# A hybrid decoder step on one core: sample and log-decay rows spread by DMA instead of one-hot matmuls, masks as Relu and 0/1 factors, squares added before their sum

## The chip, the core and the metric

The kernel runs on one core of one Trainium2 chip. The metric is the device time of one execution, in microseconds; the figure for the kernel before is the median of three runs.

## What is computed

One inference step of a two-layer decoder (D = 1024) for a prompt of 512 tokens and 8 samples of one token each. Each layer normalises x, makes one combined input projection, runs three recurrent branches on it (A: retention, B: mLSTM, C: SSD), gates and projects their sum back, then does cross-attention over 256 memory tokens and an MLP of width 4096. The prompt goes through the recurrences in chunks of 128 tokens; the samples are one state update and one read-out per head:

```python
# mLSTM, one chunk (retention has a constant decay, SSD has exp(cum_t - cum_s) in place of it)
logw = where(causal, b[t] - b[s] + i[s], -inf)
m_t  = maximum(b + m, max_s(logw))
sc   = (q @ k.T) * exp(logw - m_t)
num  = sc @ v + (q @ C) * exp(b + m - m_t)
C    = C * w_prev + (k * w_s).T @ v
# SSD, one chunk
seg  = where(causal, exp(cum_t - cum_s), 0)
y    = ((C_ @ B.T) * seg * dt_s) @ x + (C_ @ S.T) * exp(cum_t)
# a sample, each branch:  S = decay * S + v k^T ;  y = S q
```

The SSD output is multiplied by silu(z) and normalised by the mean of its squares over each group of 256 features. All arithmetic is fp32.

## The kernel before

**Layout and projections.** Activations lie feature-major: 128 features on the partitions, 520 columns (512 prompt tokens, 8 samples). Every large projection is done with fp32 split in a high and a low part. A weight chunk of 128 x 1024 (512 KB) is loaded into one of two `raw` buffers (L245), ScalarE copies its high part into `wh` (L255), VectorE subtracts to get `wl` (L256), and TensorE then runs 48 matmuls of 260 columns on it (`mmacc`, L169). `wh` and `wl` have two buffers each, so the split of a chunk starts when TensorE has finished the chunk two before it.

**Order of the work.** TensorE's order is written by hand. The mixer's per-head work sits in Python generators (`Stream`): `g_int_R`, `g_int_M`, `g_int_S` for the prompt (tile names with `Ri.`, `Mi.`, `Si.`), `g_smp_R`, `g_smp_M`, `g_smp_S` for the samples (`Rs.`, `Ms.`, `Ss.`). The projections pull them along: `mm()` advances a virtual clock by each matmul's length, and a generator that says `yield t` is resumed when that clock has moved by t microseconds. So a `yield` sets how much projection work TensorE does between two steps of a head. The other engines and the DMAs get their order from the tile scheduler's priorities. All DMAs, weights and states, loads and stores, are issued from SyncE's one queue (SP), in order; a DMA that has to wait holds up those behind it.

**Rows spread over partitions.** Three places need one row of numbers on all 128 partitions, and all three use TensorE with a one-hot stationary matrix (`sel`, `sel_b`, L629) that copies one row of the moving operand to all partitions of a PSUM tile:

- the decays. `RW` (L208) holds the rows -m_t of the four mLSTM heads and cum_t of the sixteen SSD heads, each as high and low part. `g_int_M` (L975 to L986) spreads a row over 512 columns, adds a mask of 0 and -1e30 by a second matmul (`idr`, `maskr`), and ScalarE makes exp of the sum with the s-term as bias; a third matmul of 384 columns feeds exp of the inter-chunk weight. `emask` in `g_int_S` (L1183 to L1192) does the first two for each of 4 heads of 4 groups. L1226 spreads two heads' rows over 64 partitions each with the table `selp`;
- the samples' q, k (or B, C) rows. `tok_rows` (L611 to L623) transposes two or four 128-column tiles, ScalarE and VectorE write high and low rows into `rows_r`, and for each sample a matmul spreads its 256 or 512 numbers (L806, L1073, L1288). VectorE then does, per sample and half, one `scalar_tensor_tensor` (state += v x k row) and one dot (state . q row), reading the row in PSUM;
- the SSD norm. `rms_cols` (L316) sums the squares of a group by matmuls with a column of ones, two 128-feature tiles one after the other.

Each layer has 4 heads in R, 4 in M, 4 groups of 4 heads in S, and 8 samples: 32 `emask` steps, 8 `g_int_M` heads, 16 pairs at L1226, 24 sample heads or groups, and 8 norms in the whole kernel.

Of the kernel before, what the change touches and what calls it, by code (L numbers as in the profile page):

```python
# [111 lines left out]
def tile_trunk(ctx: ExitStack, tc: tile.TileContext, I, O):  # L112
# [87 lines left out]
    mstage = tl(un, [128, 520], "row", 2)  # L200
    ld.dma_start(out=mstage[:, :128], in_=I["mask"])
    maskr = const.tile([128, 128], F32R, name="maskr")
    V.tensor_copy(out=maskr, in_=mstage[:, :128])
    idr = const.tile([128, 128], F32R, name="idr")
    V.tensor_copy(out=idr, in_=ident)

    sel = const.tile([128, 2, 32], F32R, name="sel")
# [216 lines left out]
    def layer(l, mp, load_x):  # L424
# [76 lines left out]
        def g_rows():  # L501
# [18 lines left out]
            V.tensor_scalar(out=RW[0:4, :], in0=mm_[:, 0:L], scalar1=-1.0, scalar2=None, op0=ALU.mult)  # L520
            V.scalar_tensor_tensor(out=RW[32:36, :], in0=mm_[:, 0:L], scalar=-1.0, in1=RW[0:4, :].bitcast(F32), op0=ALU.mult, op1=ALU.subtract)
# [1319 lines left out]
```

## Time and profile before

| | us |
|---|---|
| median of 3 runs (lowest, highest) | 3051.62 (3044.17, 3051.88) |
| the profiled execution | 3048.6 |
| its span from first to last instruction | 3046.8 |
| TensorE busy | 2987.1 (98%), 23708 matmuls |
| VectorE, ScalarE, GpSimd busy | 1909.3 (63%), 1241.2 (41%), 117.9 (4%) |
| DMA, queue of the loads and stores | 389.29 MB, 40.5% of 16 engines |

The chain of waits that ended last runs through TensorE for 94% of the span. The mixer, where the change lies, fills about 65 to 800 us and 1690 to 2550 us of the span. Two matmuls that follow each other overlap in the trace, so what one costs is read from start to start, not from its duration.

### The profile page before, as it was taken

The numbers are of one execution on the slowest core, as the hardware profiler recorded it, in microseconds if no ns is written. First come the engines' busy times: TensorE is split into PE (matmuls) and PEld (weight loads), VectorE is DVE, ScalarE is ACT, GpSimd is POOL, SyncE is SP. The second block draws the span as 40 slices with busy tenths as digits, with TensorE's granted clock in tenths as the row PEclk, the third lists the DMA queues.
The fourth block names the chain that finished last, engine by engine and source line by source line (L and its number), as shares of the span: only waits on it lengthen the run. The fifth ranks groups of instructions, "written<-read, shape, count | busy, mean of one in ns | idle before, by whom it ended". The sixth has DMA issues, their size and how long they took to land.

```text
span 3046.8 us, 57809 instructions
## 1 busy us (share of the span) xinstructions
PE 2987.1 (98%) x23708; PEld 2912.3 (96%) x23708; DVE 1909.3 (63%) x4460; ACT 1241.2 (41%) x2070; POOL 117.9 (4%) x384
## 2 busy tenths in 40 slices
PE   7999999999999999999999999999999999999998
PEld 7999999999999889999999999999999997899997
DVE  7677646766755765444577775567767557644445
ACT  5334444544433343322353454445444334332322
POOL 0001000100000000000000000000000000000000
PEclk9999999999999999999999999999999999999998
DMA  6334534433444642223353344444334446422322
GB/s 211 122 127 145 149 102 146 140 116 113 133 134 143 218 149 91 91 91 96 116 177 129 120 140 148 131 127 125 115 116 131 136 146 208 132 91 91 97 91 77
DMA packets 128537, 392.99 MB, mean 129 GB/s; under 512 B 16784, under 2 KB 27664, under 8 KB 128272
## 3 DMA queue, kind: packets, MB, share of 16 engines
q1 hardware_dynamic: 128272, 389.29, 40.5%
q8 instruction: 187, 3.06, 0.4%
q14 instruction: 78, 0.64, 0.1%
HBM read 331.68 MB, written 57.56 MB: 128 GB/s over the span
## 4 chain that ended last, share of the span: by engine, by line
PE 94%; DVE 2%; DMA 2%; ACT 1%; issue 0%; SPq 0%; ACTq 0%; DVEq 0%
PE mlp.pp L169 24%; PE br.pp L169 12%; PE Sp.pp L169 9%; PE Mp.pp L169 9%; PE Rp.pp L169 8%; PE br2.pp L169 6%; PE Si.pa L169 4%; PE out.pp L169 3%; PE Qp.pp L169 3%; PE wo.pp L169 3%; PE Mi.pa L169 3%; PE kv.pp L169 2%; PE Ap.pa L169 2%; PE Mp.pa L169 2%; PE Ri.pa L169 1%; PE Mi.pa L176 1%
## 5 line engine op out<-in xcount | busy, mean ns | idle before, releaser
L255 ACT ACTIVATE mlp.wh<-mlp.raw 128x1024 fp32r<-128x1024 f32 x127 | 134.8, 1061 | 485.5 <-PE mlp.pp L169 469.1
L169 PE MATMUL mlp.pp<-mlp.h,mlp.wh 128*128 128x260 f32 x2048 | 327.6, 282 | 0.0
L169 PE MATMUL mlp.pp<-kv.y,mlp.wh 128*128 128x260 f32 x1984 | 318.3, 282 | 0.0
L169 PEld LDWEIGHTS mlp.pp<-mlp.h,mlp.wh 128*128 128x128 f32 x2048 | 278.7, 188 | 0.0
L169 PEld LDWEIGHTS mlp.pp<-kv.y,mlp.wh 128*128 128x128 f32 x1984 | 270.2, 188 | 1.0 <-issue 1.0
L169 PE MATMUL mlp.pp<-mlp.h,mlp.wl 128*128 128x260 f32 x1024 | 205.0, 281 | 0.0
L169 PE MATMUL mlp.pp<-kv.y,mlp.wl 128*128 128x260 f32 x992 | 198.6, 281 | 0.0
L256 DVE TENSOR_TENSOR mlp.wl<-mlp.raw,mlp.wh 128x1024 fp32r<-128x1024 f32 x127 | 155.7, 1226 | 19.3 <-ACT mlp.wh L255 10.4
L1618 DVE SCALAR_TENSOR_TENSOR mlp.cc<-mlp.pp,rb.Cst 128x520 f32<-128x520 f32 x64 | 44.8, 700 | 188.3 <-PE mlp.pp L169 183.8
L169 PEld LDWEIGHTS mlp.pp<-mlp.h,mlp.wl 128*128 128x128 f32 x1024 | 157.4, 188 | 0.0
L169 PEld LDWEIGHTS mlp.pp<-kv.y,mlp.wl 128*128 128x128 f32 x992 | 152.5, 188 | 0.0
L169 PE MATMUL Rp.pp<-mlp.h,Rp.wh 128*128 128x260 f32 x736 | 120.5, 286 | 2.2 <-DVE Rp.ext L661 2.2
L256 DVE TENSOR_TENSOR Mp.wl<-Mp.raw,Mp.wh 128x1024 fp32r<-128x1024 f32 x56 | 68.5, 1224 | 85.2 <-ACT Mp.wh L255 85.2
L169 PE MATMUL Rp.pp<-h,Rp.wh 128*128 128x260 f32 x736 | 120.5, 286 | 1.3 <-DVE Rp.ext L661 1.3
L169 PE MATMUL Sp.pp<-mlp.h,Sp.wh 128*128 128x260 f32 x640 | 107.0, 290 | 0.0
L169 PE MATMUL Sp.pp<-h,Sp.wh 128*128 128x260 f32 x640 | 105.8, 288 | 0.0
L169 PEld LDWEIGHTS Rp.pp<-mlp.h,Rp.wh 128*128 128x128 f32 x736 | 101.1, 188 | 2.9 <-issue 2.4
L169 PE MATMUL Mp.pp<-mlp.h,Mp.wh 128*128 128x260 f32 x640 | 103.8, 284 | 0.0
L169 PE MATMUL Mp.pp<-h,Mp.wh 128*128 128x260 f32 x640 | 103.8, 284 | 0.0
L169 PEld LDWEIGHTS Rp.pp<-h,Rp.wh 128*128 128x128 f32 x736 | 101.1, 188 | 2.0 <-issue 1.5
L255 ACT ACTIVATE br.wh<-br.raw 128x1024 fp32r<-128x1024 f32 x64 | 67.6, 1056 | 82.8 <-PE br.pp L169 69.6
L1632 DVE TENSOR_TENSOR out.ucp<-mlp.pp,out.ucp 128x520 f32<-128x520 f32 x64 | 44.8, 700 | 80.6 <-PE mlp.pp L169 79.1
(799 smaller groups left out, 7981.3 us busy)
## 6 DMA issues: line engine op xcount, KB each, us to landing
mlp.raw<-wall SPq DMA_DIRECT2D x127, 512.0 KB, 3.4
br.raw<-wall SPq DMA_DIRECT2D x64, 512.0 KB, 3.5
Mp.raw<-wall SPq DMA_DIRECT2D x56, 512.0 KB, 3.5
Rp.raw<-wall SPq DMA_DIRECT2D x48, 512.0 KB, 3.5
Sp.raw<-wall SPq DMA_DIRECT2D x48, 512.0 KB, 3.5
kv.raw<-wall SPq DMA_DIRECT2D x33, 512.0 KB, 5.1
Ms.st<-s_ml SPq DMA_DIRECT2D x32, 512.0 KB, 3.5
o_mlC_s<-Ms.st SPq DMA_DIRECT2D x32, 512.0 KB, 2.9
```

The costliest lines, as they stand in the source:

```text
L169: PE.matmul(out, lhsT=lhsT, rhs=rhs, start=start, stop=stop)
L176: PE.transpose(out=out, in_=in_, identity=identity)
L255: A.activation(out=hi, in_=t, func=AF.Copy)
L256: V.tensor_tensor(out=lo, in0=t, in1=hi.bitcast(F32), op=ALU.subtract)
L1618: V.scalar_tensor_tensor(out=h2(rt), in0=ps, scalar=0.0, in1=h2(rbox[0]), op0=ALU.max, op1=ALU.mult)
L1632: V.tensor_tensor(out=h2(xs_.t[j]), in0=ps[:, :, :HF], in1=h2(xs_.t[j]), op=ALU.add)
```

## The change

Rows -m_t and cum_t are written to device memory (`rscr`) once per layer, and a DMA that repeats one row for 128 partitions (`row_bcast`, 256 KB into SBUF) takes the place of the one-hot matmul. ScalarE then does Relu of (row + bias), four times, and one Exp with scale -1; the mask is a factor 0/1, folded into `cbs` by VectorE for SSD, and applied by GpSimd's `affine_select` for mLSTM. A head's sample rows are written to device memory (`smp_scr`: one transpose of all, a copy by ScalarE, a DMA), and each `smp_bcast` DMA spreads 512 numbers of one row, or of two samples, over 128 partitions (256 KB, three buffers `bc`). VectorE reads them in SBUF. The rows of L1226 come by two DMAs of 64 partitions. The squares of SSD's two tiles are added by GpSimd before one round of `rms_cols`. The virtual-clock delays change with it. The attention's samples still use `tok_rows` and `sel_b`.

```diff
+    rscr = dram.tile([DEPTH, 20, L], F32, name="rscr")
+    sscr = dram.tile([DEPTH, 3, 4, NB * 512], F32, name="sscr")
+    def row_bcast(l, r, c0=0):
+        t = tl(un, [128, 512], "bcE", 2)
+        ld.dma_start(out=t[:, c0:L], in_=rscr[l, r, c0:L].partition_broadcast(128))
+        return t
...
+        def smp_scr(kind, h, src, n, scale=1.0):
+            ps = pa()
+            tr(out=ps[:, 0:128], in_=src, identity=ident)
+            rt = tl(sm, [128, 128], "rowt", 2)
+            A.activation(out=rt[0:NB * n, :], in_=ps[0:NB * n, 0:128], func=AF.Copy, scale=scale)
+            st_.dma_start(out=sscr[l, kind, h, 0:NB * n * 128].rearrange("(r f) -> r f", f=128), in_=rt[0:NB * n, :])
+        def smp_bcast(kind, h, b0, nb, w):
+            t = tl(un, [128, nb, w], "bc", 3)
+            ld.dma_start(out=t.rearrange("p a b -> p (a b)"), in_=sscr[l, kind, h, b0 * w:(b0 + nb) * w].partition_broadcast(128))
+            return t
...
@@ g_smp_R @@
-            r = tok_rows(qks)
+            smp_scr(0, h, qkw, 2)
...
-            yield 3.69
+            bcs = [smp_bcast(0, h, 2 * q, 2, 256) for q in range(2)]
+            yield 7.0
...
@@ g_int_M @@
-            ps = pa([128, NC, 128])
-            mm(ps.rearrange("p a b -> p (a b)"), lhsT=sel_b(h), rhs=RW, start=True, stop=False)
-            mm(ps, lhsT=idr, rhs=maskr.unsqueeze(1).to_broadcast([128, NC, 128]), start=False, stop=True)
+            mb = row_bcast(l, 16 + h)
+            yield 2.5
             E = tl(un, [128, NC, 128], "E", 2)
             for c in range(NC):
-                A.activation(out=E[:, c, :], in_=ps[:, c, :], func=AF.Exp, bias=colT[:, c, 0, h:h + 1])
-            wb = pa()
-            mm(wb[:, 0:384], lhsT=sel_b(h), rhs=RW[:, 128:512], start=True, stop=True)
+                A.activation(out=E[:, c, :], in_=mb[:, c * C:(c + 1) * C], func=AF.Relu, bias=colT[:, c, 0, h:h + 1])
+            A.activation(out=E, in_=E, func=AF.Exp, scale=-1.0)
+            G.affine_select(out=E, in_=E, pattern=[[0, NC], [1, C]], compare_op=ALU.is_ge, fill=0.0, base=0, channel_multiplier=-1)
...
@@ g_smp_M @@
+            smp_scr(1, h, qkmw[:, h * 32:h * 32 + C], 4)
             while h and not msmps[h - 1].done:
                 yield 0.5
-            r = tok_rows([t[:, (2 * h + i) * NB:(2 * h + i) * NB + C] for t in (qmw, kmw) for i in range(2)])
...
-            yield 2.3
+            bcs = [smp_bcast(1, h, b, 1, 512) for b in range(2)]
+            yield 7.0
...
-                    bc = pa()
-                    mm(bc, lhsT=sel_b(b), rhs=r, start=True, stop=True)
+                    bc = bcs.pop(0)
+                    if b < 6:
+                        bcs.append(smp_bcast(1, h, b + 2, 1, 512))
...
@@ g_int_S @@
+            eps = {r: row_bcast(l, 4 * g + r) for r in range(2)}
...
-            A.activation(out=cbs, in_=ps, func=AF.Copy, scale=0.25)
+            V.scalar_tensor_tensor(out=cbs, in0=ps, scalar=0.25, in1=mask.unsqueeze(1).to_broadcast([128, NC, 128]), op0=ALU.mult, op1=ALU.mult)
...
-                mm(ep.rearrange("p a b -> p (a b)"), lhsT=sel_b(hd, 1), rhs=RW, start=True, stop=False)
-                mm(ep, lhsT=idr, rhs=maskr.unsqueeze(1).to_broadcast([128, NC, 128]), start=False, stop=True)
                 E = tl(un, [128, NC, 128], "E", 2)
                 for c in range(NC):
-                    A.activation(out=E[:, c, :], in_=ep[:, c, :], func=AF.Exp, bias=colT[:, c, 3, hd:hd + 1])
+                    A.activation(out=E[:, c, :], in_=ep[:, c * C:(c + 1) * C], func=AF.Relu, scale=-1.0, bias=colT[:, c, 3, hd:hd + 1])
+                A.activation(out=E, in_=E, func=AF.Exp, scale=-1.0)
                 V.tensor_tensor(out=E, in0=E, in1=cbs, op=ALU.mult)
...
+                ebs = tl(un, [128, T], "yb", 2)
+                for q in range(2):
+                    ld.dma_start(out=ebs[64 * q:64 * q + 64, 0:384], in_=rscr[l, 2 * j + q, 128:512].partition_broadcast(64))
...
-                eb = pa()
-                mm(eb[:, 0:384], lhsT=selp[0][:, j * 128:(j + 1) * 128], rhs=RW[:, 128:512], start=True, stop=True)
...
-            yield 7.3
-            d = diag_cols(rms_cols(sqs, 1, 4 * EPS))
+            G.tensor_tensor(out=sqs[0], in0=sqs[0], in1=sqs[1], op=ALU.add)
+            yield 8.3
+            d = diag_cols(rms_cols(sqs[:1], 1, 4 * EPS))
...
@@ g_smp_S @@
-            r = tok_rows(bcs, 0.5)
+            smp_scr(2, g, bcs, 2, 0.5)
...
-            yield 6.67
+            bcq = [smp_bcast(2, g, 2 * q, 2, 256) for q in range(2)]
+            yield 8.0
```

Three places show how instructions move. First TensorE in SSD's prompt part, at the third head of a group (`Si.pa` is PSUM, `RW,sel` the spread row, `maskr,idr` the mask, `Sp.pp` a projection). Before:

```order
L169 MATMUL Si.pa_1151_7578<-Si.E_1117_7344,Si.ktok_1093_7173 64x128 [waits DVE_49]
L169 MATMUL Si.pa_1151_7578<-Si.E_1117_7344,Si.ktok_1093_7173 64x128 x3
L169 MATMUL Si.pa_1152_7583<-RW_107,sel_95 128x512 [waits DVE_49,PE_49]
L169 MATMUL Si.pa_1152_7583<-maskr_91,idr_93 128x512
L169 MATMUL Sp.pp_1148_7549<-h_13_141,Sp.wh_1130_7455 128x260 x4
L169 MATMUL Sp.pp_1148_7549<-h_13_141,Sp.wl_1131_7456 128x260 x2
```

With the change, from the same product of `Si.E` and the tokens on:

```order
L169 MATMUL Si.pa_1159_7543<-Si.E_1125_7298,Si.ktok_1096_7132 64x128 [waits Activation_49]
L169 MATMUL Si.pa_1159_7543<-Si.E_1125_7298,Si.ktok_1096_7132 64x128 x3
L169 MATMUL Sp.pp_1156_7514<-h_12_135,Sp.wh_1138_7421 128x260 x4
L169 MATMUL Sp.pp_1156_7514<-h_12_135,Sp.wl_1139_7422 128x260 x2
L169 MATMUL Sp.pp_1156_7514<-h_13_136,Sp.wh_1138_7421 128x260 x4
L169 MATMUL Sp.pp_1156_7514<-h_13_136,Sp.wl_1139_7422 128x260 x2
```

The pair of 512-column matmuls is gone from behind the products; only projection stands between them. Second, SyncE's queue around the samples of the first M head (`wall` is the weights, `s_ml` the states in, `o_mlC_s` out). Before:

```order
L245 DMA Mp.raw_575_3599<-wall 128x1024 [waits DMAHW5_49,DMAHW3_49,DVE_49]
L245 DMA Mp.raw_597_3718<-wall 128x1024 [waits DMAHW4_49,DVE_49]
L1080 DMA o_mlC_s<-Ms.st_546_3444 128x1024 [waits DVE_49]
L1061 DMA Ms.st_579_3619<-s_ml 128x1024 [waits DMAHW7_49,DMAHW0_49,DVE_49]
L892 DMA mscr_110<-br.th_529_3359 128x520 [waits DVE_49]
L245 DMA Mp.raw_613_3817<-wall 128x1024 [waits DMAHW5_49,DMAHW2_49,DVE_49]
L1080 DMA o_mlC_s<-Ms.st_547_3448 128x1024 [waits DVE_49]
```

With the change (`sscr` is the scratch, `bc` the spread rows, `bcE` a decay row):

```order
L239 DMA Mp.raw_569_3538<-wall 128x1024 [waits DMAHW1_49,DVE_49]
L378 DMA Mi.bcE_821_5326<-rscr_104 128x512 [waits DMAHW4_49,Activation_49]
L378 DMA Mi.bcE_970_6386<-rscr_104 128x512 [waits Activation_49]
L639 DMA sscr_105<-Ms.rowt_546_3410 32x128 [waits Activation_49]
L644 DMA Ms.bc_550_3423<-sscr_105 128x512 [waits DMAHW7_49,DMAHW6_49]
L644 DMA Ms.bc_551_3425<-sscr_105 128x512 [waits DMAHW0_49]
L644 DMA Ms.bc_565_3521<-sscr_105 128x512
L239 DMA Mp.raw_591_3654<-wall 128x1024 [waits DMAHW2_49,DVE_49]
L644 DMA Ms.bc_573_3557<-sscr_105 128x512 [waits DMAHW7_49,DMAHW3_49,DVE_49]
L1105 DMA o_mlC_s<-Ms.st_548_3415 128x1024 [waits DMAHW4_49,DVE_49]
L644 DMA Ms.bc_581_3594<-sscr_105 128x512 [waits DMAHW5_49,DMAHW0_49,DVE_49]
L644 DMA Ms.bc_584_3620<-sscr_105 128x512 [waits DMAHW1_49,DVE_49]
```

One write and six spread loads (here with two decay rows ahead) now stand around one weight load `Mp.raw`; the first load from `sscr` waits for the write before it, and later ones for VectorE to free a buffer. Third, VectorE at the start of the same head's samples. Before, the first update waits for TensorE, and the weight split `br.wl` comes soon behind:

```order
L621 SCALAR_TENSOR_TENSOR rows_r0_103<-Ms.pa_544_3435,rows_r0_103 8x512 [waits Activation_49]
L1076 SCALAR_TENSOR_TENSOR Ms.st_546_3444<-Ms.pa_548_3476,Ms.vs_545_3442,Ms.st_546_3444 128x256 [waits DMAHW5_49,DMAHW4_49,PE_49]
L628 ISA Ms.junk_549_3479,sp.ys_107_608<-Ms.st_546_3444,Ms.pa_548_3476 128x256 [waits DVE_49]
L628 ISA sp.ys_107_608 128x1
L256 TENSOR_TENSOR br.wl_553_3488<-br.raw_551_3485,br.wh_552_3487 128x1024 [waits DMAHW4_49,Activation_49]
L1076 SCALAR_TENSOR_TENSOR Ms.st_546_3444<-Ms.pa_548_3476,Ms.vs_545_3442,Ms.st_546_3444 128x256
```

With the change, the split comes first and the updates wait for the spread loads:

```order
L250 TENSOR_TENSOR br.wl_558_3460<-br.raw_556_3457,br.wh_557_3459 128x1024 [waits DMAHW2_49,PE_49,Activation_49]
L1101 SCALAR_TENSOR_TENSOR Ms.st_548_3415<-Ms.bc_550_3423,Ms.vs_547_3413,Ms.st_548_3415 128x256 [waits DMAHW7_49]
L1101 SCALAR_TENSOR_TENSOR Ms.st_548_3415<-Ms.bc_550_3423,Ms.vs_547_3413,Ms.st_548_3415 128x256
L650 ISA Ms.junk_566_3524,sp.ys_106_602<-Ms.st_548_3415,Ms.bc_550_3423 128x256 [waits DVE_49]
L650 ISA sp.ys_106_602 128x1
L1101 SCALAR_TENSOR_TENSOR Ms.st_548_3415<-Ms.bc_551_3425,Ms.vs_547_3413,Ms.st_548_3415 128x256 [waits DMAHW0_49]
```

The wait of the first update is now for a DMA from SP's queue, and no sample work waits for TensorE.

## Rows read from the trace of the kernel before

**Rows 1.** The page, part 1: busy time, share of the span, instructions.

```profile
PE 2987.1 (98%) x23708; PEld 2912.3 (96%) x23708; DVE 1909.3 (63%) x4460; ACT 1241.2 (41%) x2070; POOL 117.9 (4%) x384
```

**Rows 2.** Windows of M, S: length, busy us by engine, clock, DMA share.

```profile
260.00:570.00 310.00, 310.00 (x2447) 304.31 (x2446) 194.74 (x492) 146.75 (x262) 21.19 (x60) 1.00 0.48 140
570.00:800.00 230.00, 230.00 (x1839) 223.49 (x1838) 164.89 (x409) 104.64 (x203) 19.49 (x71) 0.99 0.37 117
```

**Rows 3.** TensorE's waits, whole span: us in total, times, longest.

```profile
PE Ap.pa L169 <- DMA Ap.pA<-kscr: 8.9, 2, 5.0
PE Mi.pa L169 <- DVE sp.ys L628: 0.6, 1, 0.6
```

**Rows 4.** The timeline of TensorE at 596 us: start, us, line, operation, count.

```profile
596.42 0.40 PE L169 MATMUL Si.pa<-RW,sel 128*128 128x512 f32 x1
596.66 0.39 PE L169 MATMUL Si.pa<-maskr,idr 128*128 128x512 f32 x1
596.88 0.64 PE L169 MATMUL br.pp<-Mi.y,br.wh 128*128 128x260 f32 x4
```

**Rows 5.** The timeline of TensorE at 602 us, spread rows of SSD samples.

```profile
602.38 0.41 PE L169 MATMUL br.pp<-Mi.y,br.wl 128*128 128x260 f32 x2
602.62 0.41 PE L169 MATMUL Ss.pa<-rows_r,sel 128*128 128x256 f32 x2
602.86 0.65 PE L169 MATMUL br.pp<-Mi.y,br.wh 128*128 128x260 f32 x4
```

**Rows 6.** The timeline of TensorE at 448 us, spread rows of mLSTM samples.

```profile
448.12 0.39 PE L169 MATMUL Ms.pa<-rows_r,sel 128*128 128x512 f32 x1
448.35 0.53 PE L169 MATMUL br.pp<-h,br.wh 128*128 128x260 f32 x3
```

**Rows 7.** The timeline of TensorE at 445 us, transposes of an mLSTM head.

```profile
444.82 0.38 PE L176 MATMUL Ms.pa<-ident,sp.qms 128*128 128x128 f32 x2
...
445.17 0.48 PE L169 MATMUL br.pp<-h,Mp.wh 128*128 128x260 f32 x2
```

**Rows 8.** The timeline of TensorE at 645 us, sums of squares of SSD.

```profile
644.85 1.84 PE L169 MATMUL Si.pa<-onesc,Si.yb 128*128 128x1 f32 x16
646.55 0.59 PE L169 MATMUL Si.pa<-Si.yb,onesc 128*128 128x8 f32 x4
647.00 0.37 PE L169 MATMUL Sp.pp<-h,Sp.wh 128*128 128x260 f32 x1
```

**Rows 9.** Groups of ScalarE by line and shape: busy us, mean ns, idle before.

```profile
L1190 ACT ACTIVATE Si.E<-Si.pa,sp.colT 128x128 f32<-128x128 f32 x128 | 36.6, 368 | 48.8 <-PE Si.pa L169 48.8
```

**Rows 10.** Groups of VectorE: SSD state updates, SBUF alone and from PSUM.

```profile
L1207 DVE TENSOR_TENSOR Si.Cst<-Si.Cst,sp.scd 128x256 f32<-128x256 f32 x24 | 10.1, 423 | 6.6 <-ACT Si.Cst L1205 6.3
L1208 DVE TENSOR_TENSOR Si.Cst<-Si.Cst,Si.pa 128x256 f32<-128x256 f32 x24 | 10.0, 416 | 8.2 <-PE Si.pa L169 8.2
```

**Rows 11.** The tile Si.E from 590 to 640 us: ns, first and last start.

```profile
L1191 DVE TENSOR_TENSOR Si.E<-Si.E,Si.qw x4: 693/693/693, 598.3 to 623.2; 128x512 f32<-128x512 f32 x4
L169 PE MATMUL Si.pa<-Si.E,Si.ktok x32: 272/273/323, 616.2 to 630.8; 128*64 128x128 f32 x32
```

**Rows 12.** Groups of GpSimd: its longest single operation.

```profile
L508 POOL MEMSET sp.st<- 128x1040 f32 x2 | 1.9, 966 | 365.6 <-DVE mlp.y L292 360.5 <-DVE y L292 5.1
```

**Rows 13.** The page, part 6: DMA issues, KB each, median us to landing.

```profile
mlp.raw<-wall SPq DMA_DIRECT2D x127, 512.0 KB, 3.4
kscr<-kv.row SPq DMA_DIRECT2D x16, 128.0 KB, 2.5
```

**Rows 14.** The page, part 5: both halves of a weight split, mean ns.

```profile
L255 ACT ACTIVATE mlp.wh<-mlp.raw 128x1024 fp32r<-128x1024 f32 x127 | 134.8, 1061 | 485.5 <-PE mlp.pp L169 469.1
L256 DVE TENSOR_TENSOR mlp.wl<-mlp.raw,mlp.wh 128x1024 fp32r<-128x1024 f32 x127 | 155.7, 1226 | 19.3 <-ACT mlp.wh L255 10.4
```

**Rows 15.** Waits of SyncE's queue: us in total, times, longest.

```profile
SPq L245 <- DVE mlp.wl L256: 642.5, 123, 5.6
```

**Rows 16.** Waits of ScalarE for state loads.

```profile
ACT Ms.st L1063 <- DMA Ms.st<-s_ml: 50.7, 18, 5.7
```

More of the change, by code (lines that the diff above doesn't have):

```diff
@@ L199, in tile_trunk @@
     V.memset(onesc[:, 1:2], 1.0 / 256.0)
[L200 to L207, printed above, removed]
+    mask = const.tile([128, 128], F32, name="mask")
+    ld.dma_start(out=mask, in_=I["mask"])
+    sel = const.tile([128, 32], F32R, name="sel")
     V.memset(sel.bitcast(F32), 0.0)
-    for b0 in (0, 32, 64, 96):
-        V.tensor_copy(out=sel[b0:b0 + 32, b0 // 64, :], in_=ident[b0:b0 + 32, b0:b0 + 32])
+    for b0 in (0, 32):
+        V.tensor_copy(out=sel[b0:b0 + 32, :], in_=ident[b0:b0 + 32, b0:b0 + 32])
     spar = const.tile([128, 136], F32, name="spar")
@@ L519, in g_rows @@
             A.activation(out=RT1[64:68, 0:L], in_=mt[:, 0:L], func=AF.Exp, scale=-1.0)
[L520 to L521 removed]
+            st_.dma_start(out=rscr[l, 16:20, :], in_=mm_[:, 0:L])
             for c in range(NC):
@@ L790, in unstash, with g_smp_R @@
             held[0] -= 1
-        def g_smp_R(h, vs, qks):
-            while not s_rows.done or (h and not smps[h - 1].done):
+        def g_smp_R(h, vs, qkw):
+            while not s_rows.done:
+                yield 0.5
+            smp_scr(0, h, qkw, 2)
+            while h and not smps[h - 1].done:
                 yield 0.5
@@ L1125, in proj_S @@
             ph[0] = "Sp."
-            if selp[0] is None:
-                sp_ = tl(un, [128, 2080], "ucp", 1, F32R)
-                G.memset(sp_[0:64, 0:1024].bitcast(F32), 0.0)
-                for q in range(2):
-                    stg = tl(un, [128, 520], "row", 2)
-                    ld.dma_start(out=stg[64:128, 0:512], in_=I["selp"][:, q * 512:(q + 1) * 512])
-                    V.tensor_copy(out=sp_[64:128, q * 512:(q + 1) * 512], in_=stg[64:128, 0:512])
-                selp[0] = sp_
             sz = tl(un, [128, 2, T], "pC", 2)
@@ L1146, in proj_S @@
             xs = tl(sm, [128, 2, NB], "xs8", 2)
-            bcw, bcs = smp_tile(2, "bc8", 2)
+            bcw, bcs = bn_tile(2, 1, "bc8", 2)
             for i in range(2):
                 G.tensor_copy(out=xs[:, i, :], in_=smp_cols(X[:, i, :]))
-                G.tensor_copy(out=bcs[:, i, :], in_=smp_cols(BC[:, i, :]))
-            return X, BC, sz, xs, [bcw[:, i * NB:i * NB + C] for i in range(2)]
+                G.tensor_copy(out=bcs[:, 0, i, :], in_=smp_cols(BC[:, i, :]))
+            return X, BC, sz, xs, bcw
         def g_int_S(g, X, BC, sz, xs, s_smp, yps):
@@ L1720, in tables @@
     s, t = np.meshgrid(np.arange(128), np.arange(128), indexing="ij")
-    r["mask"] = np.where(t >= s, 0.0, -1e30).astype(f32)
+    r["mask"] = (t >= s).astype(f32)
     half = 64
```

97 lines of the change are left out of this document (47 added, 50 removed).

## The prediction

> **What bounds the kernel now.** I read the page first: TensorE is busy 98% of the span, VectorE 63%, GpSimd 4% [rows 1]. A share over the span says little of a stage, so next the windows of the mLSTM and SSD stages of layer 0: TensorE is busy 310.0 of 310 us and 230.0 of 230, at the full clock, while VectorE has 194.7 and 164.9 and the DMA engines less than half [rows 2]. Then TensorE's waits: the only one put down to sample work is 0.6 us, once, and the largest on a transfer is 8.9 us in two waits on `kscr`, the one scratch in device memory that TensorE itself reads back, in the attention [rows 3]. So TensorE's instruction stream sets the mixer's time: a matmul less there is time less, and anything added elsewhere counts only if it makes TensorE wait. Where a distance on the timeline is used, it is from start to start.
>
> **What TensorE loses.** (1) A spread row and its mask, two matmuls of 512 columns, take 596.88 - 596.42 = 0.46 us [rows 4]. There are 32 in `emask` and 8 in `g_int_M`: 40 x 0.46 = 18.4. (2) Rows of 384 columns: two of 260 take 0.24 [rows 5], so 384 take 0.12 x 384/260 = 0.18. There are 8 in `g_int_M` and 16 at L1226: 24 x 0.18 = 4.3. (3) Sample rows in R and S: two of 256 columns take 602.86 - 602.62 = 0.24 [rows 5]; 4 pairs a head or group, 16 of these: 64 x 0.24 = 15.4. In M one of 512 takes 0.23 [rows 6], 64 of them: 14.7. (4) Transposes: four take 445.17 - 444.82 = 0.35 [rows 7]. R and S go from two to one a head, M from four to one: 40 fewer x 0.0875 = 3.5. (5) The norm: 16 passes with the column of ones and 4 for the samples take 647.00 - 644.85 = 2.15 [rows 8]; half of them goes, 8 x 1.07 = 8.6. No matmul is added. Sum: 18.4 + 4.3 + 15.4 + 14.7 + 3.5 + 8.6 = **64.9 us**, 2.1%.
>
> **What the others get.** *ScalarE*: four Exp of a row in PSUM take 368 ns each [rows 9]; now four Relu and a 512-wide Exp. A wider operand only adds to 0.37, and four times that is a ceiling: 0.4 to 1.5 us more an `emask`, nearer 0.6. The cover: VectorE's mask product at 598.3 is first read by TensorE at 616.2 [rows 11], 17 us later. I cost it at nothing; without cover it would be 40 x 0.6 = 24. *GpSimd*: eight selects of 512 and eight sums of 520 elements, which no row shows. Below stands the memset of 1040 elements, 0.97 us [rows 12], halved for half the elements; above, three such for reading two operands, 3 us. I take 1.2, near the memset. The select has cover: between the mask's product and its first use in TensorE `g_int_M` yields 2.2 + 4.12 + 4.88 = 11.2 us. The sum stands before the norm's matmuls, whose `yield` grew by 1.0 us, so 0.2 us late at worst by my value, 2 us by the upper end: 0 to 16 us in all, taken as 0 since VectorE and ScalarE feed it early. *VectorE*: the cast copies of `tok_rows` go, the 0/1 mask moves a 512-wide product from ScalarE to it, and its sample operations now read SBUF only. An update of the same shape takes 423 ns from SBUF and 416 from PSUM [rows 10]: no change.
>
> The Trainium skill speaks against that last step: its page "SBUF — State Buffer" (section "Who interferes with whom") says that a VectorE instruction with two SBUF inputs shares a read port with GpSimd, and that of the two the later fully waits. The 423 against 416 was measured with GpSimd almost idle, so no row here shows the rule at work. By the row the sum stays as it is; what it would be by the rule at its worst is the fourth rival.
>
> *SyncE's queue*: per head a write, then spread loads; in all 24 writes, 128 sample loads, 40 decay rows, 32 of 64 partitions, 4 writes of `rscr`. A write of 128 KB lands in 2.5 us and a load of 512 KB in 3.4 [rows 13]; I take 2.5 for the small writes and 2.8 for a 256 KB load, between them. That a load reads one row 128 times no row shows: from 2.5 up to any length, which is the second rival.
>
> The delicate step is the queue's order. SyncE stands waiting 642.5/123 = 5.2 us for VectorE to free a weight buffer at nearly every load [rows 15]. A sample write queues behind that; the first spread load waits for the write, and the next weight load stands behind it. From transpose to first row that makes 0.4 (copy) + 0 to 5.2 + 2.5 + 2.8 = 5.7 to 10.9 us, against a `yield` of 7.0 (S: 8.0). Late rows hold no matmul, since samples no longer touch TensorE; they hold VectorE, in whose queue weight splits stand behind the updates. The split has room: a chunk of 48 matmuls lasts 48 x 0.12 = 5.8 us [rows 5], ScalarE starts the split when TensorE releases the buffer, and both halves take 1.06 + 1.23 [rows 14], which leaves 5.8 - 2.3 = 3.5. A lateness of 0 to 3.9 us overdraws that by 0 to 0.4; I take 0.15 for each of 24 heads and groups: **3.6 us**. That a late load in front of an in-order engine need not reach TensorE, the trace shows: ScalarE waits 50.7 us for states, up to 5.7 at a time [rows 16], and TensorE does not.
>
> **Sum.** 3048.6 (the profiled execution: span 3046.8 and 1.8 around it) - 64.9 + 3.6 = 2987.3. That execution lies 3.0 below the median of the runs shown, so 2990 against 3051.6.
>
> **Rivals.** *Late rows eat the slack.* VectorE is 72% busy in SSD [rows 2], so half the 3.5 may already be used. With 1.7 left, a lateness spread evenly over 0 to 3.9 costs (2.2 x 2.2/2)/3.9 = 0.6 us a head, 15 in all, and the full lateness each time 24 x 2.2 = 53: 3002 to 3040, the middle about 3015. For it: five to seven DMAs stand between weight loads. Against: weight loads wait for VectorE there anyway.
>
> *Slower: SyncE's queue becomes the bound.* The later spread loads wait for VectorE to free one of three buffers, VectorE waits for the loads, and weights stand behind both; TensorE then waits for weights as it waits for the scratch now, 8.9/2 = 4.5 us [rows 3]. Once for each of 24 heads and groups: 107 us, 3048.6 - 64.9 + 107 + 3 = 3094. It turns the sign from 64.9/24 = 2.7 us a head on. For it: that wait is a write and a read back, the same pattern. Against: there TensorE reads the loaded tile itself; here two buffers of weights stand between.
>
> *VectorE fills the freed time.* If its in-order work set the pace of the stages, TensorE would idle where its matmuls were: about 3049. Taking half of S's share, some 17 us, from the second window leaves VectorE at 165/213 = 77%, no bound.
>
> *GpSimd and VectorE hold each other up.* 768 sample operations of about 0.42 us are 323 us, a fifth of the mixer's 1600. GpSimd's 118 us [rows 1] and 16 new operations of about 1 meet them for a fifth of 134: 27 us more on VectorE; were all of it passed on, 3017. This is the skill's rule on the shared port at its worst; passing all of it on needs a VectorE without slack.
>
> **How the numbers follow.** The forecast has 0.64, late rows 0.20, the queue 0.08, GpSimd 0.05, VectorE's pace 0.03. A measurement of this kernel can tell about 0.3%, 9 us, from no change. Forecast, GpSimd and nearly all of the late rows lie below 3042: faster 0.88. VectorE's pace and the tail of the late rows: same 0.04. The queue: slower 0.08. For the range: the prices of TensorE are read to 0.02 in 0.24, 8%, so 5 us; with no stall, and for a run at the lower end of the runs shown, 2978. Upward it takes in GpSimd and most of the late rows, to 3025; left out are the queue, VectorE's pace and the top of the late rows, together 0.18.
>
> **What would show it.** Right: about 64.9 us less TensorE busy time or more (durations overlap), no group `RW,sel`, `maskr,idr` or sample `rows_r,sel` in the mixer, TensorE's waits in the mixer below 5 us, VectorE's waits for `bc` loads tens of us without TensorE waiting. Late rows: TensorE waits for `wl` of one to two us, close behind the first update of a head. The queue: TensorE's waits name `wh` or `wl`, ScalarE's name weight loads. GpSimd: the same updates clearly longer than now, and GpSimd's copies too. The forecast is wrong if TensorE waits over 20 us in the mixer, or if TensorE's busy time falls by much less than the sum.

## The result and the profile after

| kernel | median us (lowest, highest) | ratio to the kernel before, 95% interval | TensorE waits us | lost at half clock us |
|---|---|---|---|---|
| before, beside the first measurement | 3051.0 (3044.2, 3051.9) | 1 | 49.7 | 12.8 |
| changed | 3011.9 (3009.9, 3015.0) | 0.9878 [0.986, 0.9895] | 71.2 | 13.3 |
| changed, measured again (e11) | 3005.0 (3001.4, 3007.0) | 0.9854 [0.9839, 0.9868] | 66.1 | 11.2 |

The change makes the kernel faster by 1.2 to 1.5%: 39 us in the first measurement, 43.5 in the second, where 61.3 had been forecast. The two columns at the right come from one profiled execution each. The waits are the idle times that the timeline of TensorE shows, summed. What is lost at half clock is, over windows of one microsecond, the sum of TensorE's busy time times (1 - granted clock): the time that the same work would have been shorter at 2.4 GHz.

The page of the changed kernel, busy time by engine:

```profile
PE 2926.3 (97%) x23292; PEld 2854.3 (95%) x23292; DVE 1878.1 (62%) x4429; ACT 1256.7 (42%) x2102; POOL 138.1 (5%) x396
```

Beside [rows 1], TensorE has 416 matmul instructions and 60.8 us less to do. At full clock that is (2987.1 - 12.8) - (2926.3 - 13.3) = 61.3 us of work. But the span went down only 38.7 (3046.8 to 3008.1), so 22.1 us of TensorE's idle time (span less busy time) are new. The windows of the two stages say where (columns as in [rows 2]). Both were full before:

```profile
260.00:570.00 310.00, 307.09 (x2443) 302.29 (x2442) 190.96 (x490) 146.90 (x263) 25.09 (x64) 0.99 0.55 172
570.00:800.00 230.00, 224.11 (x1802) 217.97 (x1800) 171.55 (x423) 116.15 (x221) 26.07 (x81) 0.99 0.49 157
```

The waits of TensorE over the whole span name what it waits for. Beside the 8.9 and 0.6 us of [rows 3]:

```profile
PE Me.pa L169 <- DVE Me.ysq L856: 10.1, 2, 5.1
...
PE Si.pa L169 <- DVE Si.E L326: 3.4, 2, 1.7
...
PE Mi.pa L176 <- ACT Mp.pA L991: 3.0, 2, 2.5
```

`Me.ysq` and `Si.E` are new, once in each layer; in the trace of before neither is waited for. Of the 17.7 us that the mixer's waits grew by (4.7 to 22.4), `Me.ysq` has 10.1, `Si.E` 3.4 and `Mp.pA` 3.0. In the second trace of the changed kernel (e11) the mixer's waits are 16.7. (Counted are 65 to 940 and 1560 to 2450 us. In the trace of before the mixer's projections start at 51 and 1555 us and its last projection ends at 936 and 2441, not at 800 and from 1690 to 2550 as the section on the time before has it.)

**The wait for `Me.ysq`.** This is `smp_norm` (from L848 on), called by `g_end_M` when all four mLSTM heads' samples are done: a mean by TensorE, a subtraction and a square by VectorE, then a sum by TensorE a fixed delay of 2.39 us later. TensorE's timeline:

```profile
567.27 0.53 PE L169 MATMUL Me.pa<-sp.ys,ones 128*128 128x32 f32 x4
...
570.36 0.46 PE L169 MATMUL br.pp<-h,Sp.wl 128*128 128x260 f32 x2
575.92 1.06 PE L169 MATMUL Me.pa<-Me.ysq,ones 128*128 128x32 f32 x4 [5.11 <-DVE Me.ysq L856]
576.80 1.21 PE L169 MATMUL br.pp<-h,Sp.wh 128*128 128x260 f32 x4
```

The sum stands some 3 us behind the mean in TensorE's order, and everything behind it waits with it. VectorE's timeline around it (the same columns), from the step that makes the mean's input, the product of `sp.ys` with `dens`:

```profile
561.43 0.22 DVE L1131 TENSOR_TENSOR sp.ys<-sp.ys,Me.dens 128x64 f32<-128x64 f32 x1
...
569.03 1.23 DVE L250 TENSOR_TENSOR Sp.wl<-Sp.raw,Sp.wh 128x1024 fp32r<-128x1024 f32 x1 [1.77 <-ACT Sp.wh L249]
...
571.23 1.62 DVE L940 SCALAR_TENSOR_TENSOR Sp.cc<-Sp.ext,cols,Sp.cc 128x552 f32<-128x552 f32 x2 [0.97 <-ACT Sp.cc L938]
...
574.25 0.22 DVE L854 SCALAR_TENSOR_TENSOR sp.ys<-Me.pa,sp.ys 128x64 f32<-128x64 f32 x1
...
575.66 0.21 DVE L856 TENSOR_TENSOR Me.ysq<-sp.ys 128x64 f32<-128x64 f32 x1
```

The mean is ready before 568, but in VectorE's order a weight split, convolution steps of SSD and state updates stand before the subtraction, and two of them wait for ScalarE. The same place in the kernel before:

```profile
564.71 0.22 DVE L1106 TENSOR_TENSOR sp.ys<-sp.ys,Me.dens 128x64 f32<-128x64 f32 x1
...
567.07 0.53 PE L169 MATMUL Me.pa<-sp.ys,ones 128*128 128x32 f32 x4
568.95 0.22 DVE L828 SCALAR_TENSOR_TENSOR sp.ys<-Me.pa,sp.ys 128x64 f32<-128x64 f32 x1
...
569.79 0.22 DVE L830 TENSOR_TENSOR Me.ysq<-sp.ys 128x64 f32<-128x64 f32 x1
...
570.39 0.53 PE L169 MATMUL Me.pa<-Me.ysq,ones 128*128 128x32 f32 x4
```

There the square was ready 0.4 us before TensorE took it (570.01 and 570.39), so the delay of 2.39 us just fitted. The rows that the samples read are not late at this place: the product ends 5.6 us ahead of the mean's matmuls in the changed kernel and 2.1 us ahead in the kernel before. What grew is the time from the end of the mean to the start of the square: 2.2 us before, 7.9 with the change (2.5 and 7.7 in the second layer).

The windows show the price, which is more than the wait (columns as in [rows 2]):

```profile
570.00:576.00 6.00, 0.89 (x8) 0.68 (x6) 4.79 (x12) 5.47 (x15) 1.01 (x6) 0.84 0.32 110
576.00:582.00 6.00, 6.00 (x32) 6.00 (x33) 5.69 (x25) 2.66 (x5) 1.56 (x5) 0.59 0.31 77
```

While TensorE stands, VectorE and ScalarE are busy (4.8 and 5.5 of 6 us). When it goes on, its granted clock is near the lower level (0.59 in the mean of these 6 us): 2.5 us lost on top of 5.1.

**The wait for `Si.E`.** At the end of the layer the last SSD group's sum of squares feeds `diag_cols`, and the branch projection of `Si.y` needs the result. TensorE's timeline:

```profile
868.09 0.37 PE L169 MATMUL Si.pa<-Si.yb,onesc 128*128 128x8 f32 x2
868.31 0.73 PE L169 MATMUL br2.pp<-h,br2.wh 128*128 128x260 f32 x4
...
871.70 1.12 PE L169 MATMUL Si.pa<-Si.E,ones 128*128 128x512 f32 x2 [1.69 <-DVE Si.E L326]
872.26 1.04 PE L169 MATMUL br2.pp<-Si.y,br2.wh 128*128 128x260 f32 x4
```

GpSimd's new sum of the squares had ended long before TensorE took it:

```profile
857.89 1.31 POOL L1269 TENSOR_TENSOR Si.yb<-Si.yb,Si.yb 128x520 f32<-128x520 f32 x1 [41.96 <-ACT Si.yb L1267]
```

857.89 + 1.31 = 859.2, while TensorE's first one-column pass starts at 867.3; in all eight groups 5.3 to 8.1 us lie between. The delay of 8.3 us ahead of the sum is longer than the sum needs, and in this kernel the last group, behind which little work is left, pays for it (with the same 8.3 us the squares alone, e2 below, have no such wait).

**What went as foreseen.** VectorE waits for the spread rows and TensorE does not wait behind it at the heads, though the transfers land later than the 2.8 us that were taken (DMA issues with KB each and median us to landing; then VectorE's groups, columns as in [rows 10]):

```profile
Ms.bc<-sscr SPq DMA_DIRECT2D x64, 256.0 KB, 4.5
...
Rs.bc<-sscr SPq DMA_DIRECT2D x32, 256.0 KB, 3.7
...
Ss.bc<-sscr SPq DMA_DIRECT2D x32, 256.0 KB, 3.6
```

```profile
L1101 DVE SCALAR_TENSOR_TENSOR Ms.st<-Ms.bc,Ms.vs,Ms.st 128x256 f32<-128x256 f32 x128 | 59.3, 480 | 24.7 <-DMA Ms.bc<-sscr 16.2 <-ACT Ms.st L1086 5.2 <-DMA mscr<-br.th 3.3
...
L1315 DVE SCALAR_TENSOR_TENSOR Ss.st<-Ss.bc,Ss.xd,Ss.st 128x128 f32<-128x128 f32 x128 | 43.7, 352 | 4.9 <-DMA Ss.bc<-sscr 4.9
```

With the 7.2 us of the retention that is 28.3 us in which VectorE waits for spread rows. No wait of TensorE names a `wl` behind them.

### The profile page after: what moved, and what is told of

The parts are those of the page before. It is cut to its first block, busy times and chain, and to the rows that moved or that the text cites. A ratio compares the mean times of both kernels' runs of the same rounds, so it can differ in the third digit from the quotient of the medians.

```text
span 3008.1 us, 57176 instructions
## 1 busy us (share of the span) xinstructions
PE 2926.3 (97%) x23292; PEld 2854.3 (95%) x23292; DVE 1878.1 (62%) x4429; ACT 1256.7 (42%) x2102; POOL 138.1 (5%) x396
## 5 line engine op out<-in xcount | busy, mean ns | idle before, releaser
L249 ACT ACTIVATE br.wh<-br.raw 128x1024 fp32r<-128x1024 f32 x64 | 67.7, 1057 | 88.0 <-PE br.pp L169 62.8
L169 PE MATMUL Mp.pp<-mlp.h,Mp.wh 128*128 128x260 f32 x640 | 104.0, 284 | 0.0
L250 DVE TENSOR_TENSOR br.wl<-br.raw,br.wh 128x1024 fp32r<-128x1024 f32 x64 | 78.3, 1223 | 30.1 <-ACT br.wh L249 29.9
```

The source lines that it names most:

```text
L169: PE.matmul(out, lhsT=lhsT, rhs=rhs, start=start, stop=stop)
L249: A.activation(out=hi, in_=t, func=AF.Copy)
L250: V.tensor_tensor(out=lo, in0=t, in1=hi.bitcast(F32), op=ALU.subtract)
```

## The experiments

All ratios are to the kernel before on the same chip; waits and losses are read as in the first table.

| run | median us | ratio, interval | waits | half clock |
|---|---|---|---|---|
| e1 norm later | 3006.0 | 0.9858 [0.9844, 0.9873] | 68.3 | 11.4 |
| e2 squares alone | 3035.3 | 0.9955 [0.994, 0.9969] | 51.8 | 8.8 |
| e3 decays alone | 3033.6 | 0.9953 [0.9937, 0.997] | 53.9 | 11.0 |
| e4 samples alone | 3034.0 | 0.994 [0.9916, 0.9964] | 63.9 | 18.8 |
| e5 no row loads | 2996.3 | 0.9825 [0.9811, 0.984] | 63.8 | 12.0 |
| e6 sum earlier | 2998.4 | 0.983 [0.9816, 0.9845] | 60.4 | 12.2 |
| e7 = e1 + e6 | 3003.4 | 0.9847 [0.9832, 0.9862] | 62.8 | 13.7 |
| e8 squares undone | 3011.1 | 0.9872 [0.9856, 0.9889] | 64.5 | 15.3 |
| e9 = e6 + rows sooner | 2999.9 | 0.9835 [0.9821, 0.985] | 57.8 | 12.6 |
| e10 = e9, retention too | 2998.1 | 0.9831 [0.9814, 0.9847] | 60.3 | 15.9 |
| e12 = e9 + norm 5.5 | 2992.4 | 0.9816 [0.9803, 0.983] | 57.1 | 9.8 |

**e1: the norm later.** Theory 1: the waits are local, because TensorE's row stands too soon behind a step of VectorE. The rival: late rows or the queue hold VectorE up.

```diff
-            yield 2.39
+            yield w
...
-            yield from smp_norm(ysm, EPS)
+            yield from smp_norm(ysm, EPS, 9.0)
```

> The changed kernel, with the second sum of the mLSTM samples' norm put 9.0 instead of 2.39 us of matmuls behind the first; nothing that VectorE does before it moves. Theory 1 (the wait is local: VectorE's in-order queue has the norm's subtraction behind weight split, conv and state products, and TensorE's order gives it 2.39 us only): the two waits of 5.1 and 5.0 us on Me.ysq go, 3012 - 10 = 3002 us, nothing else grows. Rival, late rows (VectorE as a whole is behind because of the spread loads): the wait turns up again a little later, 3009 to 3012 us.

Measured 3006.0. The waits for `Me.ysq` are gone, and others stand in their place:

```profile
PE Mi.pa L176 <- DVE Si.qw L1196: 6.6, 2, 3.9
PE Si.pa L169 <- DVE Si.E L326: 3.4, 2, 1.7
...
PE br.pp L169 <- ACT Sp.ext L931: 1.6, 1, 1.6
```

Of the 10.1 us, 6.6 - 0.5 are now waited for at `Si.qw` and 1.6 at `Sp.ext`: moving TensorE's row does not make VectorE and ScalarE faster in that stretch. Beside the changed kernel's two measurements (0.9878, 0.9854) the gain is open. The time decides neither theory; the timeline above has the wait where theory 1 puts it.

**e2, e3, e4: the three parts alone**, each put into the kernel before.

```diff
@@ e2 @@
-            yield 7.3
-            d = diag_cols(rms_cols(sqs, 1, 4 * EPS))
+            G.tensor_tensor(out=sqs[0], in0=sqs[0], in1=sqs[1], op=ALU.add)
+            yield 8.3
+            d = diag_cols(rms_cols(sqs[:1], 1, 4 * EPS))
@@ e3: all of rscr, row_bcast and the masks @@
-            mm(ps.rearrange("p a b -> p (a b)"), lhsT=sel_b(h), rhs=RW, start=True, stop=False)
+            mb = row_bcast(l, 16 + h)
...
@@ e4: all of sscr, smp_scr and smp_bcast @@
-            r = tok_rows(qks)
+            smp_scr(0, h, qkw, 2)
...
```

> The kernel before, with only the squares of SSD's two tiles added by GpSimd and one round of sums (delay 8.3 for 7.3). By the price of the prediction 8 x 1.07 = 8.6 us less, 3051 - 8.6 = 3042; if the later sum is what makes TensorE wait 1.7 us for the diagonal in each layer, 3046. Rival (a matmul of one column frees less than its distance on the timeline): 3047 to 3051 without such a wait.

> The kernel before, with only the decay rows by DMA and the masks as factors; samples by matmul, squares unadded. By price 18.4 + 4.3 = 22.7 us less: 3028. Theory 1: no wait on the spread rows anywhere, some us at the norm of the mLSTM samples if VectorE's order has the subtraction late here too: 3028 to 3036. Rival, queue: waits for weights at the loads of 40 + 32 rows, over 3036.

> The kernel before, with only the sample rows by DMA; decays by matmul, squares unadded. By price 15.4 + 14.7 + 3.5 = 33.6 us less: 3017. Theory 1: about 10 us given back at the norm of the mLSTM samples, under 5 elsewhere: 3027 to 3032. Rival, late rows or queue: waits of TensorE for weights or PSUM at many of 24 heads, over 3032, and the sum of the three parts falls short of the whole change by more than 5.

Measured 13.1, 14.8 and 14.4 us less than before; together 42.3, about what the whole change gives. TensorE's work at full clock (busy less what the half clock costs, from the pages and the tables) falls by 2974.3 - (2976.2 - 8.8) = 6.9, 2974.3 - (2965.7 - 11.0) = 19.6 and 2974.3 - (2959.6 - 18.8) = 33.5 us, where 8.6, 22.7 and 33.6 had been priced. So the largest term is the one that is not paid out: the samples take 33.5 us off TensorE and bring 14.4, for TensorE waits 14.2 us more and loses 6.0 more at half clock. Their waits stand in no other part alone (e4, TensorE's waits; its lines are some 7 further down):

```profile
PE Me.pa L169 <- DVE Me.ysq L863: 6.5, 2, 4.2
PE Mp.pp L169 <- ACT Mp.pB L976: 4.6, 2, 2.4
```

The squares alone bring more than their work, 7 us below what was expected: the falls of the clock behind the old sums are gone (e8). Their profiled execution, the slowest of four, has 4.0 us less lost at half clock and 2.1 more of waits, so 9 of the 13.1 are accounted for. The decays came out in the range of theory 1, but not by the norm: there VectorE takes the subtraction right behind the mean, and their largest new wait is 3.9 us for `Mi.ysb`. The samples alone lie 2 us above theory 1 and just inside the rival's time, without the waits at many heads that the rival asks for.

**e5: no row loads.** Takes away the cause that the rival names.

```diff
-            st_.dma_start(out=sscr[l, kind, h, ...], in_=rt[0:NB * n, :])
-            t = tl(un, [128, nb, w], "bc", 3)
-            ld.dma_start(out=t..., in_=sscr[l, kind, h, ...].partition_broadcast(128))
-            return t
+            return bcc.rearrange("p (a b) -> p a b", a=nb)
```

> The changed kernel, but the sample rows are neither written to device memory nor loaded back: VectorE's sample work reads one constant tile instead, so the samples' outputs leave out their rows. VectorE's 28.3 us of waits for those loads (16.2 + 4.9 + 7.2) and 13 MB per layer of SyncE's transfers go away. Theory 1 (the new waits sit where TensorE's row stands too early behind a step of VectorE or ScalarE, whatever the loads do): within 7 us of the changed kernel, 3005 to 3015, the 3.4 us for the last squares sums still there and the waits for Me.ysq still over 2 us together. Rival (rows that come late, or a queue full of spread loads, hold the samples and through them TensorE): 2988 to 2998, the waits for Me.ysq gone, TensorE's waits below 57 us.

Measured 2996.3, within the rival's time. `Me.ysq` has left the list of TensorE's waits; `Si.E` is still there:

```profile
PE Si.pa L169 <- DVE Si.E L326: 3.4, 2, 1.7
```

So "whatever the loads do" falls for `Me.ysq`: without the loads the square starts 2.1 us behind the mean, as before the change. For `Si.E` theory 1 stands. The sum of waits, 63.8, missed the rival's "below 57", and the traffic that went away is 33.8 MB, 17 a layer and not 13. But e5 does not show that the rows come late. In this kernel the scheduler also orders VectorE's steps anew: the product of `sp.ys` with `dens` ends at 540.8, in the changed kernel at 561.7, and the subtraction starts 1.8 us behind the mean instead of 6.5. In both kernels the product is done before the mean starts, by 24.6 and 5.6 us.

**e6: the sum earlier.**

```diff
-            yield 8.3
+            yield 4.3
             d = diag_cols(rms_cols(sqs[:1], 1, 4 * EPS))
```

> The changed kernel with the delay before the SSD's squares sum cut from 8.3 to 4.3 us, so that TensorE's row of one-column passes stands about 4 us earlier; GpSimd's sum ended 5.3 to 8.1 us before it was taken. Theory 1: TensorE's waits for Si.E by the last group's sum (1.7 us in each layer) go or shrink, 3 to 5 us less, 3007 to 3009, unless the waits move on as in the run with the later norm (then 3010 to 3012). Rival: GpSimd's add is not ready at the earlier place (wait of TensorE on Si.yb in several of 8 groups), 3012 to 3020.

Measured 2998.4, 6.6 us below the better of the changed kernel's two measurements and more than was expected. TensorE, last group of layer 0:

```profile
858.95 0.95 PE L169 MATMUL Si.pa<-onesc,Si.yb 128*128 128x1 f32 x8
859.76 0.37 PE L169 MATMUL Si.pa<-Si.yb,onesc 128*128 128x8 f32 x2
...
865.81 1.02 PE L169 MATMUL Si.pa<-Si.E,ones 128*128 128x512 f32 x2
866.26 1.05 PE L169 MATMUL br2.pp<-Si.y,br2.wh 128*128 128x260 f32 x4
```

No wait is left, nor any on `Si.yb`. From SSD's last projection to this point it takes 865.8 - 809.1 = 56.7 us where the changed kernel takes 871.7 - 812.3 = 59.4: 2.7 us in each layer, 5.4 in all, against either trace of the changed kernel. The rest (in its trace a shorter second `Me.ysq` and no `Mp.pA`) is within what the changed kernel's own two traces differ by.

**e7: both.**

> The changed kernel with the mLSTM samples' norm later (delay 9.0 for 2.39) and the squares sum earlier (4.3 for 8.3): both repairs in one. If they act apart: 3006 less 3 = 3003, with no wait of TensorE on Me.ysq and none on Si.E over 0.5 us. If the local lag of VectorE and ScalarE only moves the wait to the next place: 3005 to 3009. Rival (the queue or late rows set the pace): 3009 to 3013.

Measured 3003.4. Neither wait is there, but TensorE now waits 7.9 us in two waits for `Si.qw`. The time is that of the first expectation, yet for the wrong reason: it is no better than e6, since the wait moved on to the next place, as in e1 and as the second expectation has it.

**e8: the squares undone.**

> The changed kernel with only the SSD's squares put back: 20 one-column passes for each group in place of 4, GpSimd's eight adds gone. By prices 8.6 us back: 3020 to 3021. If the granted clock's falls right behind those sums belong to the 20 passes, three or four of them (after the sums of the groups whose next row is full of matmuls) are in the trace again at 1.7 us each, and the time is 3023 to 3028. Rival (the falls of the clock come from elsewhere and only happened to stand there): no fall at these places, 3018 to 3021, and if GpSimd's adds held VectorE up, below 3018.

(The 20 passes are 16 of one column and 4 of eight; with the squares added there are 8 and 2.) Measured 3011.1, between nothing and 6 us above the changed kernel's two measurements, so inside the whole change the squares bring little or nothing as they stand. With the old delay of 7.3 us the waits for `Si.E` fall from 3.4 to 0.3, and TensorE's waits are 6.7 us fewer than in the first trace of the changed kernel, 1.6 fewer than in e11's; that pays for part of the passes or for all of them. Both times expected were too long; the clock's part was seen. TensorE in the kernel before, where nothing waits:

```profile
718.89 1.84 PE L169 MATMUL Si.pa<-onesc,Si.yb 128*128 128x1 f32 x16
720.59 0.59 PE L169 MATMUL Si.pa<-Si.yb,onesc 128*128 128x8 f32 x4
721.04 0.73 PE L169 MATMUL Sp.pp<-h,Sp.wh 128*128 128x260 f32 x4
...
723.02 1.07 PE L169 MATMUL Sp.pp<-h,Sp.wh 128*128 128x260 f32 x4
```

Windows of before there, then of e8 behind its first sum (at 638.8), then of the changed kernel around its sum at 645.9:

```profile
720.00:722.00 2.00, 2.00 (x19) 2.00 (x19) 0.68 (x5) 1.68 (x4) 0.47 (x3) 1.00 0.00 0
722.00:724.00 2.00, 2.00 (x12) 2.00 (x11) 1.93 (x6) 0.00 (x0) 0.00 (x0) 0.50 0.01 4
```

```profile
639.00:641.00 2.00, 2.00 (x20) 2.00 (x19) 1.03 (x2) 0.85 (x1) 1.18 (x3) 1.00 0.09 18
641.00:643.00 2.00, 2.00 (x11) 2.00 (x12) 2.00 (x5) 0.00 (x0) 0.00 (x0) 0.54 0.73 276
```

```profile
644.00:648.00 4.00, 4.00 (x37) 4.00 (x36) 2.71 (x5) 2.22 (x4) 1.40 (x4) 1.00 0.25 77
```

TensorE is busy all the time, and right behind 20 narrow passes the granted clock is 0.50: four matmuls of 260 columns take 0.87 us (the next one starts at 723.89), where at 716 us they take 0.48. That follows 4 of 8 sums in before, 3 of 8 in e8 and e3, 4 of 8 in e4, and none of the 8 sums of half the passes in any of the other ten traces, e2's and the changed kernel's among them. Each fall costs 1.7 us.

**e9, e10: the rows sooner.**

```diff
             bcs = [smp_bcast(1, h, b, 1, 512) for b in range(2)]
-            yield 7.0
+            yield 3.0
```

(with e6's edit; e10 also has 3.69 for 7.0 in `g_smp_R`)

> The run with the earlier squares sum (4.3), and in the mLSTM's sample work the delay between the issue of the first spread loads and their use cut from 7.0 to 3.0 us. Each head waits for the head before, so the fourth ends up to 4 x 4 = 16 us earlier. Theory 3, formed after the run without the loads (the samples' chain of heads was made longer by the change, its norm comes late and TensorE's row is queued behind it): TensorE's 7.6 us of waits for Me.ysq go, and some 2 to 3 us at half clock behind them: 2986 to 2993. Theory 1 (only the order of VectorE's steps at the norm): 2996 to 3001, waits for Me.ysq still over 2 us. Rival: the first rows are then not there, VectorE's waits for Ms.bc grow from 18 to over 28 us and hold up what stands behind: over 3002.

> As the run before it, and the retention's sample delay cut from 7.0 to 3.69 us (that of the kernel before) as well. No wait of TensorE on the retention's norm stands in any trace, so by theory 3 nothing is gained there: within 3 us of the run before it. Rival: those samples too delay what VectorE does for TensorE in the retention stage (waits for Rp.ext and Rs.st, some 2 to 3 us): 2 to 5 us less.

Measured 2999.9 and 2998.1, the same as e6. The samples come sooner, the mean (554.6 instead of 562.8 in e6) and the square (560.3 instead of 571.4) too, and the wait is shorter, not gone:

```profile
557.82 0.40 PE L169 MATMUL Sp.pp<-h,Sp.wl 128*128 128x260 f32 x2
560.59 1.06 PE L169 MATMUL Me.pa<-Me.ysq,ones 128*128 128x32 f32 x4 [2.37 <-DVE Me.ysq L856]
```

With 1.52 in the second layer that is 3.9 for 7.6. The fall of the clock is as dear behind 2.4 us as behind 5.1 (3.2 us lost here), so the time did not follow, and theory 3's time was wrong. Nor does its cause fit: the rows now come just as the mean wants them (the product ends 0.06 us before it, and the mean itself waits 0.44 us for it), while in e6 they were 5.4 us ahead, and yet the wait is shorter here. What got shorter is the way from the end of the mean to the start of the square, 5.1 us for 8.1: VectorE's order at the norm. VectorE's waits for `Ms.bc` did not grow (15.1 us). The retention's delay costs nothing, as expected.

**e11: the changed kernel again.**

> The changed kernel once more, beside the two above: 3009 to 3015. Its own first trace has a wait of 2.5 us on Mp.pA at 330 us and 1.7 us at half clock behind it, while five kernels with the same order up to there show 0.2 to 1.0 us: if that was chance it is under 1 us here; the waits for Me.ysq (5.1 and 5.0) and for Si.E (1.7 twice) belong to the order and stay within 1 us.

Measured 3005.0, on its lower side outside what was expected. The first wait for `Mp.pA` is 0.25 us here, so the 2.5 does not belong to the order; `Si.E` is 1.70 and 1.71 again; `Me.ysq` 4.9 and 3.2, so the second is less fixed than was expected.

**e12: three repairs**: e9, and the norm's delay 5.5 instead of 2.39.

> The run with the rows sooner, and the delay between the square and the sum in the mLSTM samples' norm 5.5 us in place of 2.39: TensorE's row of the sum stands some 3 us later, behind the next six projection matmuls and five of the mLSTM, and VectorE's square does not move. Waits for Me.ysq of 2.37 and 1.52 us go, and the 3.2 and 1.7 us at half clock behind them with them if no other wait over 2 us takes their place: ratio to the kernel before lower by 0.0013 (waits alone) to 0.003 than the 0.9835 of the run with the rows sooner, about 2991 to 2996. Rival (the waits move on to Sp.ext, Sp.wl or Si.qw, as when the norm alone was put later): no gain, 0.983 to 0.985, 2997 to 3001.

Measured 2992.4, as expected, and the best of all: 57 us below before. TensorE's sum of the norm, and the largest wait left in that stretch:

```profile
560.82 1.03 PE L169 MATMUL Mi.pa<-Mi.Cst,Mi.qw 128*128 128x257 f32 x4
561.68 0.53 PE L169 MATMUL Me.pa<-Me.ysq,ones 128*128 128x32 f32 x4
562.05 0.73 PE L169 MATMUL Sp.pp<-h,Sp.wh 128*128 128x260 f32 x4
...
573.00 0.51 PE L169 MATMUL br.pp<-h,br.wl 128*128 128x260 f32 x2 [1.19 <-DVE br.wl L250]
```

```profile
556.00:576.00 20.00, 18.65 (x146) 17.95 (x146) 16.90 (x60) 15.38 (x40) 2.42 (x13) 1.00 0.37 111
```

The sum waits for nothing, the square comes 5.1 us behind the mean as in e9, and the clock stays at 1.00. That sets it apart from e7, whose stretch from 571 to 587 us has 6.1 us of waits, 3.9 of them in one, and 2.5 us lost at half clock behind it. Here five waits from 555 to 583 us make 3.7, none over 1.2, and nothing is lost.

## Why the prediction was right in sign and 22 us too good

**The work taken off TensorE: right, 6% high.** Priced at 64.9, it measured 61.3 at full clock (by chance the same figure as the forecast gain). The samples' 33.6 and the measured 33.5 agree; decays and squares were 3.1 and 1.7 too dear.

**The stalls: the step that failed.** 3.6 us were put down for late rows; the idle time grew by 22.1. The shortfall, 22.6 between the forecast gain of 61.3 (64.9 - 3.6) and the span's 38.7, is the 18.5 by which the idle time exceeds the 3.6, and 4.1 by which the busy time fell short of 64.9. The sentence that failed is "Late rows hold no matmul, since samples no longer touch TensorE". They do still touch it: at the end of the mLSTM branch `g_end_M` sends their result through a norm whose sums are TensorE's, the second at a place fixed by a delay of 2.39 us behind the first. What TensorE waits for there is VectorE, in whose order SSD's split, convolution and state steps stand between the mean and the subtraction: the square starts 7.9 us behind the mean for 2.2 before. The part with the samples alone has this wait, those with decays or squares alone do not (e2 to e4), without the loads it is gone (e5), and a sum put later does not wait for it (e1, e12). It is not lateness of the rows: they are done 5.6 us ahead of the mean. The prediction looked for lateness at `wl`, close behind a head's first update; there none came: the room of 3.5 us that it worked out for the split held. The rival "late rows eat the slack" came near the time (its middle was 3015) by luck: its sign, waits for `wl` of one to two us behind a head's first update, is in neither trace of the changed kernel. That the measured time lies within the range is luck in the same way: the range was drawn for late rows and GpSimd, and other waits filled it. (Its lower end does not come out of its own terms: 3044.2 - 64.9 - 5 is 2974, not 2978. Nothing here hangs on it.)

**GpSimd's sum: the size right, the delay missed.** It takes 1.31 us for an assumed 1.2, the select 0.63, and neither makes TensorE wait. The prediction compared the added 1.0 us of `yield` with GpSimd's time and took 0 from its range of 0 to 16. It did not ask what the delay itself costs the last group: 3.4 us of waits with 8.3, 0.3 with the old 7.3 (e8), and 5.4 us less time with 4.3 (e6).

**A wait costs more than its length.** No term stood for the clock. Two entries nearly cancel here: the falls behind the old sums are gone, 4 x 1.7 = 6.8 us, and four others come behind waits of the mixer (at 331, 575, 1564 and 2058 us, 7.9 in all), so the total lost is 13.3 for 12.8 (the rest, 6.0 before and 5.4 after, lies in the attention and at the end). Three of these waits are new or longer; the one at 1564, 2.1 us for `Rp.ext`, stood in before too, with no fall behind it.

**ScalarE's cover held.** Four Relu of 390 ns and an Exp of 626 are 2.19 for 4 x 0.368 = 1.47 [rows 9]: 0.71 us more a step, the 0.6 foreseen, and no wait of TensorE names it.

**VectorE: no change, and the Trainium skill's rule is small here.** The sample operations went from 477 to 480, 347 to 352 and 345 to 347 ns, the dots from 416 to 419, 284 to 291 and 283 to 290, in all some 3 us over 768 operations where the fourth rival had 27. What the Trainium skill says of the shared read port ("SBUF — State Buffer", section "Who interferes with whom") is not seen beyond that. On the other side GpSimd's 272 copies take 111.1 us in sum for 104.0 before; with the samples alone, the part that gives VectorE its second SBUF input, they take 105.6. Single groups of copies move by more and both ways, and no run isolates what stretches them. At 5% of the span it costs no time.

**SyncE's queue: not the bound.** Landing was mis-sized (3.6 to 4.5 us for 2.8), but TensorE's waits name no `wh` or weight load in the mixer. The forecast's own test said it is wrong if TensorE waits over 20 us in the mixer: it waits 22.4, and 16.7 in the second trace; the sign of being right, below 5, is missed in both.

What stays open: why VectorE's order has the subtraction so far behind the mean. It comes with the samples' part (e4) and goes with the loads (e5), but each of these moves the delays, the transfers or the whole order at once; no run changed VectorE's order at the norm alone. Nor was a second queue for the row loads tried.
